# Wider weight units in a second mixer, and its last retention beside the output projection

## The chip, the cores and the metric

The kernel runs on one core of a Trainium2 chip. The metric is the device time of one execution in microseconds (us), as the median of several runs. One further execution is recorded by the hardware profiler; its trace gives the start and the length of every instruction on every engine: TensorE (PE, with its weight loads as PEld), VectorE (DVE), ScalarE (ACT), GpSimd (POOL), and SyncE (SP), which issues most of the transfers.

## What is computed

Two transformer blocks, one after the other, on 512 tokens of 1024 channels, in float32. The first block has a feed-forward, a mixer that ends in a product with `w_o`, and a second feed-forward. The second block has a mixer of latent attention and retention, and a layer of retrieved experts (`peer`). The change lies in the mixer of the second block; of the first block it touches the product with `w_o` alone.

```python
def hybrid_mixer(...):
    ...
    z = jax.nn.sigmoid(g_a) * (o_a @ w_up_a) + jax.nn.sigmoid(g_b) * (o_b @ w_up_b)
    return z @ w_o

def second_block(...):
    h = rms_norm_2(x, g_norm1[l]) * (1.0 + sc1) + sh1
    proj = h @ w_in[l]        # q_lat 256, kv_lat 128, k_rope 32, rq, rk, rv, rg 512 each
    y_mla = mla_group(q_lat, kv_lat, k_rope, ...)
    y_ret = retention_group(rq, rk, rv, rg, positions, g_ret_norm[l])
    mixed = jnp.concatenate([y_mla, y_ret], axis=-1) @ w_out[l]
    x = x + gt1 * mixed
    h2 = rms_norm_2(x, g_norm2[l]) * (1.0 + sc2) + sh2
    x = x + gt2 * peer(h2, ...)

def retention_group(q, k, v, gate, ...):     # 8 heads of 64, 4 chunks of 128 tokens
    ...
    scores = jnp.einsum('bnihd,bnjhd->bnhij', qc, kc) * dmask
    y_inner = jnp.einsum('bnhij,bnjhd->bnihd', scores, vc)
    ...                                      # states: prev of chunk n from chunks 0..n-1
    y_cross = jnp.einsum('bnihk,bnhkv,hi->bnihv', qc, prev, xi)
    y = (y_inner + y_cross)                  # then normalised per head, times silu(gate)
```

## The kernel before

**Products.** A float32 operand is held as a pair of rounded parts, high and low, and `mm3` (L124) makes a product of two such pairs with three matmuls (L126, L127, L128). Weights arrive by a transfer on SP's queue (`raw`, L109, two buffers) and are made into pairs by `split` (L116): ACT writes the high part (L120), DVE the low part (L121). Three pairs of 1024 columns are held at a time. Activations are turned by TensorE (`transposed`, L403, transposes in L414) and then made into pairs by `to_pair` (L130).

**Token tiles and banks.** The 512 tokens are four tiles of 128. PSUM has eight banks of 512 columns. They are dealt into rings: in the second mixer `ps` has four banks, `sc` two and `po` two (`self.banks(ps=4, sc=2, po=2)`). A tile of a ring is free again when its last reader is done.

**Dense units.** `nform` (L552) computes a unit: the token tile's transposed rows stand still, up to 256 weight columns stream past them, 8 steps over the 1024 channels, for the four token tiles in their four `ps` banks; then `then(t, p)` takes a bank's result away. `late` are two callbacks of the boundary before it, with which the last two token tiles are normalised and turned while the first products run.

**The second mixer** (`mixer2`, L1044). `mla` (L1077) computes the latents in two units (k latent with the rotated key part, 160 columns in a unit padded to 256; then the query latent, 256), norms and turns them, forms keys, values and queries, and does the causal attention (`heads_attend`, L925). Between its steps stand three units of the retention (`more`): values and gates of the heads' first half, values of the second half. The rest is the retention, done by halves of four heads. `ret_part` (L1136) is one unit of 256 columns (part 0 queries, 1 keys, 2 values, 3 gates); queries and keys are rotated (`rope`, L575), turned and put away. `ret_mix` does one half: the states of three chunks (L1188 to L1197), then for each chunk of 128 tokens the scores (L1207, masked in L1210), the output from the states (L1219, 64 rows of operand) and from the scores (L1220, 128 rows), alternating by head, squares (L1224), and the scaled output (L1232). `merge` (L635) runs the first half's `ret_mix` between the units of the second half (`ret_project`). The second half's `ret_mix` has beside it only the turning of the attention's output. After it all of PSUM is dealt into one ring, the retention's output is turned, and `project` does the output projection.

**Projection** (`project`, L1015). Eight half-units (512 channels by 256 columns). The first two are multiplied for all token tiles at once; the other six are kept as pairs, and `boundary` (L435) then finishes one token tile after the other: its products, the residual (L1633), the norm, and its transposes for the next layer. The first mixer's `w_o` goes through the same function. Its input `z` is made in eight rows, which come in the order 4, 5, 0, 6, 1, 7, 2, 3 (`combine1`, L965).

**Order.** What runs on one engine runs in an order that is fixed when the program is built: a scheduler takes the instruction that is ready first by its own estimate, and among those the one that stands first in the program.

## Time and profile before

| what | value |
|---|---|
| time, median of 3 runs | 2857.19 us (2850.86 to 2858.55) |
| profiled execution, its own time | 2857.06 us |
| its span in the trace | 2855.3 us |
| mean granted TensorE clock over the span | 0.987 of full speed |
| PE, PEld busy | 2786.9 us (98%), 2394.8 us (84%) |
| DVE busy | 2063.3 us (72%) |
| ACT busy | 1159.0 us (41%) |
| POOL busy | 368.6 us (13%) |

An engine's busy time is the sum of its instructions' times, and a share is of the span. The second mixer with its projection lies from about 1302 to 1598 us of the span. The granted clock is told as a share of the full 2.4 GHz: 1.00 is 2.4 GHz, 0.50 is 1.2 GHz, and a mean between them says that a stretch had both. A matmul's recorded time is that from its start to its end in the pipeline; what it costs in a run is the distance from its start to the start of the next.

### The profile page before, as it was taken

To read this page: it belongs to the slowest core of one execution; us is meant where nothing else is said; L and a number is where in the kernel's file an instruction comes from. 1 tells how busy PE (TensorE), PEld (TensorE's weight loads), DVE (VectorE), ACT (ScalarE), POOL (GpSimd) and SP (SyncE) were. 2 spreads that over 40 slices of the span, in tenths; PEclk is the share of its full clock that TensorE was granted. 3 is DMA by queue.
4 is the path that set the end of the run, shared out by engine and by line. 5 is a ranking of instruction groups with operands and counts; after the bars stand their busy time and mean duration, and the time that the engine had idled before them with its cause. 6 is when DMAs were issued, how large, how long until landed. Compare 5 with 4: busy or idle time off the path is not lost. (4 is left out here: it accounts for less than half of the span.)

```text
span 2855.3 us, 40921 instructions
## 1 busy us (share of the span) xinstructions
PE 2786.9 (98%) x15565; PEld 2394.8 (84%) x15565; DVE 2063.3 (72%) x4448; ACT 1159.0 (41%) x1930; POOL 368.6 (13%) x367
## 2 busy tenths in 40 slices
PE   8999999999999999999999999999999999999998
PEld 6877778869788877888898888999988888899996
DVE  6895257785656787226664789999967778887887
ACT  4343144333534444225522433655633333333333
POOL 0000000000000000001001002111121115443441
PEclk9999999999999999999997999999999999999999
DMA  6663221212033554321121226888899999888894
GB/s 274 224 232 140 94 84 60 93 60 89 16 139 139 188 225 178 110 103 42 67 79 47 103 90 216 310 281 309 322 333 338 327 313 362 314 311 319 295 334 189
DMA packets 152533, 553.08 MB, mean 194 GB/s; under 512 B 12368, under 2 KB 61840, under 8 KB 112400
## 3 DMA queue, kind: packets, MB, share of 16 engines
q1 hardware_dynamic: 111040, 404.25, 38.8%
q0 software_dynamic: 38848, 140.56, 13.8%
q10 hardware_dynamic: 2448, 5.65, 0.5%
q8 instruction: 122, 2.00, 0.3%
q14 instruction: 75, 0.61, 0.1%
HBM read 505.95 MB, written 44.47 MB: 193 GB/s over the span
## 5 line engine op out<-in xcount | busy, mean ns | idle before, releaser
L120 ACT ACTIVATE whi<-raw 128x1024 fp32r<-128x1024 f32 (+2 forms) x491 | 510.3, 1040 | 806.5 <-PE ps L127 377.3
L121 DVE TENSOR_TENSOR wlo<-raw,whi 128x1024 fp32r<-128x1024 f32 (+2 forms) x491 | 588.7, 1199 | 294.2 <-ACT whi L120 289.4
L126 PE MATMUL ps<-h_hi,whi 128*128 128x384 f32 (+2 forms) x1904 | 691.5, 364 | 4.6 <-ACT ga L1443 3.3
L127 PE MATMUL ps<-h_lo,whi 128*128 128x384 f32 (+2 forms) x1904 | 684.4, 360 | 0.9 <-DVE h_lo L132 0.9
L128 PE MATMUL ps<-h_hi,wlo 128*128 128x384 f32 (+2 forms) x1904 | 683.1, 359 | 1.6 <-DVE wlo L121 1.6
L126 PEld LDWEIGHTS ps<-h_hi,whi 128*128 128x128 f32 x1904 | 359.4, 189 | 37.7 <-ACT ga L1443 4.2
L128 PEld LDWEIGHTS ps<-h_hi,wlo 128*128 128x128 f32 x1904 | 359.1, 189 | 33.7 <-DVE wlo L121 2.4
L127 PEld LDWEIGHTS ps<-h_lo,whi 128*128 128x128 f32 x1904 | 359.7, 189 | 31.5 <-DVE h_lo L132 1.3
L126 PE MATMUL acc<-whi,wh 128*128 128x512 f32 x768 | 303.9, 396 | 1.6 <-ACT wh L131 1.6
L128 PE MATMUL acc<-whi,wl 128*128 128x512 f32 x768 | 303.9, 396 | 0.3 <-DVE wl L132 0.3
L127 PE MATMUL acc<-wlo,wh 128*128 128x512 f32 x768 | 303.7, 396 | 0.0
L1458 POOL DMA_INDIRECT erow<-in_eu,ids x128 | 142.8, 1116 | 649.3 <-DVE junk L1462 478.1
L131 ACT ACTIVATE wh<-wv 128x384 fp32r<-128x384 f32 x128 | 67.1, 524 | 339.4 <-issue 174.2
L1458 POOL DMA_INDIRECT erow<-in_ev,ids x128 | 166.7, 1302 | 222.7 <-DVE eacc L1470 197.0
L126 PE MATMUL ps<-whi,h_hi 128*128 128x256 f32 (+1 forms) x608 | 187.3, 309 | 0.0
L127 PE MATMUL ps<-wlo,h_hi 128*128 128x256 f32 (+1 forms) x608 | 185.3, 305 | 0.0
L128 PE MATMUL ps<-whi,h_lo 128*128 128x256 f32 (+1 forms) x608 | 185.2, 305 | 0.0
L128 PEld LDWEIGHTS acc<-whi,wl 128*128 128x128 f32 x768 | 144.5, 188 | 36.0 <-DVE wl L132 0.8
L126 PEld LDWEIGHTS acc<-whi,wh 128*128 128x128 f32 x768 | 144.3, 188 | 35.1 <-ACT wh L131 1.9
L127 PEld LDWEIGHTS acc<-wlo,wh 128*128 128x128 f32 x768 | 144.4, 188 | 32.9
L1470 DVE SCALAR_TENSOR_TENSOR eacc<-erow,wgt,eacc 128x1024 f32<-128x1024 f32 x127 | 162.7, 1281 | 4.0 <-DMA erow<-in_ev,ids 2.3
L285 DVE SCALAR_TENSOR_TENSOR rows<-mraw,sil,rows 128x256 f32<-128x256 f32 x336 | 160.3, 481 | 6.6
(457 smaller groups left out, 4602.9 us busy)
## 6 DMA issues: line engine op xcount, KB each, us to landing
raw<-in_euT SPq DMA_DIRECT2D x64, 1024.0 KB
raw<-in_evp SPq DMA_DIRECT2D x64, 1024.0 KB
raw<-in_gu SPq DMA_DIRECT2D x44, 1024.0 KB
mraw<-in_wmod SPq DMA_DIRECT2D x24, 1024.0 KB
mraw<-in_wada SPq DMA_DIRECT2D x24, 1024.0 KB
dg<-gb SPq DMA_DIRECT2D x24, 1024.0 KB
gt<-dg SPq DMA_DIRECT2D x16, 1536.0 KB
raw<-in_dn SPq DMA_DIRECT2D x22, 1024.0 KB
```

The source lines that it names most:

```text
L120: self.nc.scalar.activation(hi, r, AF.Copy)
L121: self.last_low = self.nc.vector.tensor_tensor(lo, r, hi.bitcast(F32), op=OP.subtract)
L126: mm(out, l[0], r[0], start=start, stop=False)
L127: mm(out, l[0], r[1], start=False, stop=False)
L128: self.last_mm = mm(out, l[1], r[0], start=False, stop=stop)
L131: self.nc.scalar.activation(hi, v, AF.Copy)
L285: nc.vector.scalar_tensor_tensor(rows, rv[:, k, :], c, rows, op0=OP.mult, op1=OP.add)
L1458: nc.gpsimd.indirect_dma_start(out=row, out_offset=None, in_=src, in_offset=bass.IndirectOffsetOnAxis(ap=ids[:, m:m + 1], axis=0))
L1470: nc.vector.scalar_tensor_tensor(eacc, row, wg[:, m:m + 1], eacc, op0=OP.mult, op1=OP.add)
```

## The change

Weights of the second mixer come in units of 416 or 512 columns, each as two halves of 512 channels (`half_units`).

- The two latent units become one of 416 columns (`latents`). The split of its last part goes into the space that later holds the values (`room`), and `cq2` and `oa2` share a space.
- The eight retention units of 256 columns become four of 512: values with gates (`ret_values`), queries with keys (`ret_queries`). Both halves' values and gates now stand inside `mla`. The rotation runs over eight heads at a time.
- `ret_mix` is split into `scores` and `outputs`. The scores of chunk n+1 come before the outputs of chunk n. An output chunk's products are grouped: scores' product of the first pair of heads, states' product of the first pair, states' product of the second pair, scores' product of the second pair. The bank rings are `sc` and `po` throughout. The states come after the first scores.
- The first half's `ret_mix` goes between the parts of the second half's query and key unit. The second half's goes beside the first quarter of the output projection (`project_start`: 512 channels of the attention by 512 columns, in eight parts of six matmuls); the retention's output is turned in the `po` banks as it comes.
- Both projections (`wo` and `wo2`) use half-units of 512 columns. In the second one `rest` turns the last token tile after the second quarter's products of the first two tiles have been put down; PSUM isn't dealt out anew.

The diff, cut to its core; most lines that go out are left out of it, since the functions before are printed above.

```diff
-            p = self.ps(tag)
+            p = self.ps(tag if isinstance(tag, str) else tag[k // 4])
...
+    def nform(self, *args, **kw):
+        for _ in self.nform_steps(*args, **kw):
+            pass
+    def nform_steps(self, units, x, width, then, kd=KD, late=None, room=None):
+        kr = kd // len(units)
+        kh = min(kr, 1024 // width)
         out = [self.ps() for _ in range(NT)]
         ws = []
+        for i, ap in enumerate(units):
+            r = self.raw(ap)
+            for k0 in range(i * kr, (i + 1) * kr, kh):
+                o = (k0 - i * kr) * width
+                end = k0 + kh == kd
+                hl = self.split(r[:, o:o + kh * width], [z[:, :kh * width] for z in room] if room and end else None)
+                ws += [(k0 + j, [z[:, j * width:(j + 1) * width] for z in hl]) for j in range(kh)]
+                if late and not end:
+                    continue
+                for t in range(NT):
+                    ts = slice(t * P, (t + 1) * P)
+                    if late and t < 2:
+                        late[t]()
+                    for k, w in ws:
+                        self.mm3(out[t][:, :width], (x[0][:, k, ts], x[1][:, k, ts]), w, k == 0, k == kd - 1)
+                    yield
+                ws = []
...
+    def project_start(self, ap, z, y):
+        r = self.raw(ap[0])
+        for i in range(2):
+            w = self.split(r[:, i * 1024:(i + 1) * 1024])
+            for t in range(NT):
+                self.project_part(z, y[t], t, 0, i, w)
+                yield
+    def project_part(self, z, o, t, u, i, w):
+        ts = slice(t * P, (t + 1) * P)
+        for j in range(2):
+            k = u // 2 * 4 + 2 * i + j
+            cs = slice(j * 512, (j + 1) * 512)
+            self.mm3(o, (z[0][:, k, ts], z[1][:, k, ts]), (w[0][:, cs], w[1][:, cs]), k == 0, k == KD - 1)
+    def project(self, ap, z, pool, join, scale, bias, y, rest=None, tags=("ps",) * NT):
         ws, room = [], []
+        for n, names in ((2, ("ath", "atl")), (1, ("bth", "btl"))):
+            q = [pool.tile([P, n, 1024], F32R, name=x, tag=x) for x in names]
+            room += [[v[:, j, :] for v in q] for j in range(n)]
+        for u in (1, 2, 3):
+            r = self.raw(ap[u])
+            for i in range(2):
+                ws.append((u, i, self.split(r[:, i * 1024:(i + 1) * 1024], room.pop(0) if len(ws) > 2 else None)))
+            if u == 1 and rest:
+                for t in range(2):
+                    for q in ws:
+                        self.project_part(z, y[t][1], t, *q)
+                rest()
+        def product(t):
+            for u, i, w in ws:
+                if not (rest and t < 2 and u == 1):
+                    self.project_part(z, y[t][u % 2], t, u, i, w)
+        return self.boundary(lambda t: join(t, y[t]), scale, bias, product, tags)
...
         oy = res.tile([P, NT, 512], F32, name="oy2")
+        x0, x1 = ({n: res.tile([P, NT, 256], F32, name=n + j) for n in "vg"} for j in "01")
+        more = [lambda: self.ret_values(0, x0, h), lambda: self.ret_values(1, x1, h)]
         with ExitStack() as s1:
+            oa = self.mla(self.pool(s1, "mla", reuse_waits="tile"), s1, res, h, late, more)
         with ExitStack() as s1:
             pool = self.pool(s1, "ret", reuse_waits="tile")
             self.ret_consts(pool)
             t1 = self.ret_tiles(pool, x1)
             with ExitStack() as s2:
                 t0 = self.ret_tiles(self.pool(s2, "ret0", reuse_waits="tile"), x0)
+                for _ in self.ret_queries(0, t0, h):
+                    pass
                 self.acol(4, 13, "g_norm2_2")
...
+                mix = self.ret_mix(0, t0, oy)
+                for n, _ in enumerate(self.ret_queries(1, t1, h)):
+                    if n % 2:
+                        next(mix, None)
+                for _ in mix:
+                    pass
             pool = self.pool(st, "turned2", side="right", reuse_waits="tile")
             mT = [pool.tile([P, KD, S], F32R, name=n) for n in ("mTh", "mTl")]
+            def turn(t):
+                self.transposed(oy[:, t, :], 4, t, *mT, self.col("g_ret_norm_2"), None, 4, tag="po")
+            for t in range(NT):
+                self.transposed(oa[:, t, :], 4, t, *mT, tag="sc")
+            y = [[self.ps()] for _ in range(NT)]
+            start = self.project_start(a["wo2"], mT, [z[0] for z in y])
+            for n, _ in enumerate(self.ret_mix(1, t1, oy)):
+                if n in (4, 6, 7):
+                    turn(n // 2 - 2 if n < 7 else 2)
+                next(start, None)
+            for _ in start:
+                pass
+        for t in range(2):
+            y[t].append(self.ps("sc"))
+        def rest():
+            turn(NT - 1)
+            for t in (2, 3):
+                y[t].append(self.ps("po"))
+        return mT, grow, y, rest, self.pool(st, "last2", reuse_waits="tile")
...
-        vv = pool.tile([P, NT, 512], F32, name="vv2")
         with ExitStack() as s2:
             prep = self.pool(s2, "prep2", reuse_waits="tile")
             pa = prep.tile([P, NT, 416], F32, name="pa2")
+            cq = res.tile([P, 4, S], F32R, name="cq2", tag="oa2")
+            cq = [cq[:, :2], cq[:, 2:]]
             ck = [prep.tile([P, 1, S], F32R, name=n) for n in ("ckh2", "ckl2")]
-            self.latents(a["wi2"][0], 160, h, pa, 0, late)
+            room = pool.tile([P, 2, 1024], F32R, name="room2", tag="vv2")
+            self.latents([a["wi2"][j] for j in range(2)], 416, h, pa, 0, late, [room[:, j, :] for j in range(2)])
+            vv = pool.tile([P, NT, 512], F32, name="vv2", tag="vv2")
             self.banks(ps=4, sc=2, po=2)
             for t in range(NT):
                 c = pa[:, t, 0:128]
                 self.normed(c, 128)
                 self.transposed(c, 1, t, ck[0], ck[1], self.col("g_kv_norm_2"), tag="sc")
-            self.latents(a["wi2"][1], 256, h, pa, 160)
-            more[0]()
-            w = self.split(self.raw(a["wl5"]))
             for t in range(NT):
                 c = pa[:, t, 160:416]
                 self.normed(c, 256)
                 self.transposed(c, 2, t, cq[0], cq[1], self.col("g_q_norm_2"), tag="sc")
+            more[0]()
+            w = self.split(self.raw(a["wl5"]))
             self.k_nope([w], 1, ck, kT)
             for t in range(NT):
                 ts = slice(t * P, (t + 1) * P)
...
+            self.q_rope(a["wl4"], 2, cq, qT, None, 4)
             more[1]()
-            self.q_rope(a["wl4"], 2, cq, qT, None, 4)
-            more[2]()
             self.q_nope(a["wl3"], 2, cq, qT)
...
+    def ret_units(self, hh, n):
+        return [self.a["wr2"][(2 * hh + n) * 2 + j] for j in range(2)]
+    def ret_values(self, hh, x, h):
+        nc = self.nc
+        def then(t, p):
+            pv = p[:, :256].rearrange("p (h e) -> p h e", e=64)
...
+            nc.scalar.activation(x["g"][:, t, :], p[:, 256:], AF.Silu)
+        self.nform(self.ret_units(hh, 1), h, 512, then)
+    def ret_queries(self, hh, x, h):
+        nc = self.nc
+        zeta = self.rc["zeta"]
+        xi = self.rc["xi"].rearrange("p (g i) -> p g i", g=4)[:, 2 * hh:2 * hh + 2]
+        def then(t, p):
             ts = slice(t * P, (t + 1) * P)
+            qr = self.misc.tile([P, 8, 64], F32, name="rr", tag="v")
+            self.rope(p.rearrange("p (h e) -> p h e", e=64), qr, 32, 4 + t, 8)
+            nc.vector.tensor_tensor(x["kz"][:, t, :].rearrange("p (h e) -> p h e", e=64), qr[:, 4:],
+                                    zeta[:, 4 * hh:4 * hh + 4, None].to_broadcast([P, 4, 64]), op=OP.mult)
             pp = self.ps("sc")
+            for g in range(4):
                 nc.tensor.transpose(pp[:, g * P:(g + 1) * P],
                                     qr[:, 2 * g:2 * g + 2, :].rearrange("p a b -> p (a b)"), self.idf)
+            pv = pp.rearrange("p (n g e) -> p n g e", g=2, e=P)
+            nc.scalar.activation(x["qT"][:, :, ts], pv[:, 0], AF.Copy)
+            nc.scalar.activation(x["kT"][:, :, ts], pv[:, 1], AF.Copy)
+            nc.vector.tensor_tensor(x["qx"][:, :, ts], pv[:, 0], xi, op=OP.mult)
+        yield from self.nform_steps(self.ret_units(hh, 0), h, 512, then)
+    def ret_mix(self, hh, x, oy):
         nc = self.nc
         st = x["st"]
         dm = self.rc["dmask"].rearrange("p (g s i) -> p s g i", g=4, s=2)[:, :, 2 * hh:2 * hh + 2]
         dec = self.rc["dec"][:, 2 * hh:2 * hh + 2]
+        half = [slice(64 * s, 64 * s + 64) for s in range(2)]
+        ats = {}
+        def scores(n):
             ts = slice(n * P, (n + 1) * P)
+            ats[n] = self.misc.tile([P, 4, P], F32, name="rat", tag="sg")
+            pst = [self.ps("sc"), self.ps("sc")]
             for g in range(2):
                 for s in range(2):
+                    nc.tensor.matmul(pst[s][:, g * P:(g + 1) * P], x["kT"][half[s], g, ts], x["qT"][half[s], g, ts],
                                      start=True, stop=True)
             for s in range(2):
+                nc.vector.tensor_tensor(ats[n][:, 2 * s:2 * s + 2, :],
+                                        pst[s][:, :256].rearrange("p (g i) -> p g i", g=2), dm[:, s], op=OP.mult)
+        def outputs(n):
+            ts = slice(n * P, (n + 1) * P)
+            at = ats.pop(n)
+            py = [self.ps("po"), self.ps("po")]
+            o = [[py[s][:, g * 64:(g + 1) * 64] for s in range(2)] for g in range(2)]
+            def inner(g, start):
+                for s in range(2):
                     hd = 2 * g + s
+                    nc.tensor.matmul(o[g][s], at[:, 2 * s + g, :], x["v"][:, n, hd * 64:(hd + 1) * 64],
+                                     start=start, stop=not n or not start)
+            def cross(g, start):
+                for s in range(2) if n else ():
+                    nc.tensor.matmul(o[g][s], x["qx"][half[s], g, ts], st[half[s], n - 1, g, :],
+                                     start=start, stop=not start)
+            inner(0, True)
+            cross(0, False)
+            cross(1, True)
+            inner(1, not n)
...
+        scores(0)
+        for n in range(3):
+            p = self.ps("po")
+            for g in range(2):
+                gs = slice(g * P, (g + 1) * P)
+                nc.tensor.matmul(p[:, gs], x["kz"][:, n, gs], x["v"][:, n, gs], start=True, stop=True)
...
+        yield
+        for n in range(NT):
+            if n + 1 < NT:
+                scores(n + 1)
+                yield
+            outputs(n)
...
-            h = self.project(a["wo"], z, pool, pn(1), 2, 6)
+            y = [[self.ps(), self.ps()] for _ in range(NT)]
+            for _ in self.project_start(a["wo"], z, [q[0] for q in y]):
+                pass
+            h = self.project(a["wo"], z, pool, pn(1), 2, 6, y)
...
-            mT, grow, pool = self.mixer2(h[0], st, h[1])
-            h = self.project(a["wo2"], mT, pool, lambda t, y: self.residual(t, y, grow), 4, 12)
+            mT, grow, y, rest, pool = self.mixer2(h[0], st, h[1])
+            h = self.project(a["wo2"], mT, pool, lambda t, y: self.residual(t, y, grow), 4, 12, y, rest,
+                             [("ps", "sc" if t < 2 else "po") for t in range(NT)])
...
+    def half_units(w, n):
+        return np.concatenate([cols_units(w[q * 512:(q + 1) * 512], n) for q in range(2)])
...
-    a["wo"] = cols_units(f["w_o"][0], 256)
+    a["wo"] = half_units(f["w_o"][0], 512)
-    a["wi2"] = cols_units(w2, 256)
+    a["wi2"] = half_units(np.concatenate([w2[:, 256:416], w2[:, :256]], 1), 416)
+    r2 = w2[:, 416:].reshape(D, 2, 2, 2, 256).transpose(0, 3, 1, 2, 4).reshape(D, 4, 512)
+    a["wr2"] = np.concatenate([half_units(r2[:, n], 512) for n in range(4)])
-    a["wo2"] = cols_units(f["w_out_2"][0], 256)
+    a["wo2"] = half_units(f["w_out_2"][0], 512)
```

## Rows read from the trace of the kernel before

**Rows 1.** page, section 1: busy us, share of span, instructions

```profile
PE 2786.9 (98%) x15565; PEld 2394.8 (84%) x15565; DVE 2063.3 (72%) x4448; ACT 1159.0 (41%) x1930; POOL 368.6 (13%) x367
```

**Rows 2.** stretches: from:to, us, busy (instructions) by engine, granted clock, DMA share, GB/s

```profile
1301.70:1322.30 20.60, 15.67 (x114) 15.47 (x113) 12.99 (x41) 11.19 (x29) 3.49 (x8) 0.83 0.14 52
1473.40:1550.90 77.50, 72.42 (x442) 64.25 (x441) 42.40 (x136) 19.04 (x40) 10.17 (x16) 0.78 0.09 32
1550.90:1597.90 47.00, 47.00 (x402) 47.00 (x401) 28.13 (x49) 19.46 (x31) 1.65 (x3) 1.00 0.27 101
```

**Rows 3.** PE's waits, 1300 to 1600: us in total, times, longest

```profile
PE ps L414 <- DVE oy L1232: 3.1, 1, 3.1
```

**Rows 4.** PE by time, latents (start, us, instruction): twelve starts apart

```profile
1328.11 0.28 PE L127 MATMUL ps<-wlo,h_hi 128*128 128x256 f32 x1
...
1329.55 0.28 PE L127 MATMUL ps<-wlo,h_hi 128*128 128x256 f32 x1
```

**Rows 5.** PE by time, second feed-forward's down projection: eight starts apart

```profile
1299.62 0.39 PE L126 MATMUL ps<-fhi,lhi 128*128 128x512 f32 x1
...
1301.44 0.39 PE L128 MATMUL ps<-fhi,llo 128*128 128x512 f32 x1
```

**Rows 6.** PE by time, last token tile's transposes at the latents, wait

```profile
1310.50 1.97 PE L414 MATMUL ps<-idf,xs 128*128 128x128 f32 x8 [4.93 <-ACT xs L448]
```

**Rows 7.** PE by time, first output projection: a wait; two starts 36 apart

```profile
875.62 0.38 PE L126 MATMUL ps<-whi,zh 128*128 128x256 f32 x1 [1.02 <-ACT zh L131]
...
880.22 0.28 PE L126 MATMUL ps<-whi,zh 128*128 128x256 f32 x1
...
884.46 0.28 PE L126 MATMUL ps<-whi,zh 128*128 128x256 f32 x1
```

**Rows 8.** PE by time, retention: merged lines (xcount) with the next start

```profile
1473.39 0.60 PE L1163 MATMUL sc<-idf,rr 128*128 128x128 f32 x4
1473.83 1.06 PE L1188 MATMUL po<-v,rkz 128*128 128x128 f32 x8
...
1481.60 0.56 PE L1220 MATMUL po<-v,rat 128*128 128x64 f32 x4
1481.97 0.36 PE L127 MATMUL ps<-wlo,h_hi 128*128 128x256 f32 x1
...
1505.10 0.69 PE L1219 MATMUL po<-rst,rqx 64*128 64x64 f32 x2
1505.71 0.69 PE L1220 MATMUL po<-v,rat 128*128 128x64 f32 x2
...
1516.99 0.71 PE L1207 MATMUL sc<-rqT,rkT 64*128 64x128 f32 x8
1517.54 0.34 PE L1219 MATMUL po<-rst,rqx 64*128 64x64 f32 x4
1517.71 0.44 PE L1207 MATMUL ps<-rqT,rkT 64*128 64x128 f32 x2
1518.21 0.43 PE L1220 MATMUL po<-v,rat 128*128 128x64 f32 x2
1518.58 0.43 PE L1219 MATMUL po<-rst,rqx 64*128 64x64 f32 x2
```

**Rows 9.** busy time of 5 us slices of the retention

```profile
1500.00:1505.00 5.00, 5.00 (x22) 4.34 (x21) 2.03 (x7) 0.28 (x1) 1.28 (x2) 0.50 0.02 3
1530.00:1535.00 5.00, 5.00 (x23) 4.24 (x23) 2.21 (x7) 0.56 (x2) 1.05 (x3) 0.54 0.00 0
```

**Rows 10.** ACT, DVE by time; DVE groups: count, busy us, mean ns

```profile
1544.63 0.28 ACT L1224 ACTIVATE ysq<-ps 128x128 f32<-128x128 f32 x1 [1.38 <-PE ps L1220]
1546.83 0.86 DVE L1232 SCALAR_TENSOR_TENSOR oy<-ps,rstd,rg 128x64 f32<-128x64 f32 x4 [1.47 <-POOL rstd L148]
...
L121 DVE TENSOR_TENSOR wlo<-raw,whi 128x1024 fp32r<-128x1024 f32 x5 | 6.1, 1220 | 0.0
L1159 DVE TENSOR_TENSOR rkz<-rr,zeta 128x256 f32<-128x256 f32 x8 | 3.4, 423 | 0.2
```

154 lines of the change are left out of this document (25 added, 129 removed).

## The prediction, made before the changed kernel had run

> **What bounds the kernel now.** I read the busy time of each engine first, then a table of stretches around the second mixer, then who TensorE (PE) waited for there, then PE's instructions in order of time, for the distance from one start to the next. PE is busy for 98% of the span [rows 1], so time goes where PE's own instructions go, or where its clock falls. The table cuts the stretch that is changed into four parts [rows 2]: the end of the feed-forward boundary with the first latent unit (20.6 us), the attention part with the second latent unit and three retention units (to 1473.4, not among the rows), the retention (77.5 us), the output projection (47.0 us). The reader is to see the third row: 72.4 us busy, but the mean granted clock is 0.78, DVE is busy for only 42.4 us, and DMA hardly at all. PE is the limit there too, with poor work: small matmuls, partly at 1.2 GHz instead of 2.4. The waits it has, the longest 3.1 us [rows 3], come to 77.5 - 72.4 = 5.1 us. After this mixer the kernel is a chain of PE work whose gathers and loads are issued by its progress; I see no transfer with a date of its own, so I let what is saved here reach the end in full.
>
> **Paces of the wide matmuls.** A start with 256 columns comes every 1.44/12 = 0.120 us [rows 4], one with 512 every 1.82/8 = 0.2275 us [rows 5]. The distance is not proportional: two narrow ones take 0.240, so joining them gives back 0.0125 us. Between the two a straight line gives 0.187 us for 416 columns (estimate). In the first mixer's output projection the narrow ones come every 4.24/36 = 0.1178 us [rows 7], so less is gained there.
>
> **Latent units (160 of 256 columns, then 256; now 416).** Before, 192 matmuls of 256 columns: 23.0 us. After, 96 x 0.187 = 18.0. On the path it is more: 24 of them for the first token tile lie ahead of the wait for the last token tile's normalised rows [rows 6], which ends when ACT and DVE are done, so they are filler there; behind it 168 x 0.120 = 20.2 become 72 x 0.187 = 13.5, -6.7 us. Four splits of 832 columns stand ahead of that chain where two of 1024 stood; one of them lies in the chain of ACT and DVE and costs between 0 and 1.0 us (1.2 us for 1024 columns [rows 10], scaled); I take 0.6. Sum -6.1. The clock after the wait is a further open point: the stretch has 0.83 [rows 2], so 0.17 x 20.6 = 3.5 us at most are lost to it. A wait shorter by 1.6 us might keep it; I count nothing, and 2.4 us in the low end. The second latent unit hid the chain of the key-value norm; now the value unit does, 21.8 us of independent matmuls, and the instructions on PE are ordered by readiness, so that costs nothing. If the value unit's splits came late (their buffers come free within the last token tile, 4.5 us, against 2.3 for a split on both engines), it would be some 2 us.
>
> **Retention units (eight of 256 become four of 512).** Each pair goes from 192 x 0.120 = 23.0 to 96 x 0.2275 = 21.8: -1.2 each, -4.8 us. The second half's gates move from the retention into the attention stretch, which changes no sum. The rotation now runs over eight heads in one instruction; DVE has half as many, of about 0.42 us [rows 10] instead of two of 0.28, and gains some. But it holds a bank of the four until its four reads are done, and then() of four token tiles takes about 10 us against 8.2 until the next unit wants the last bank: a wait of about 1.5 us, counted below.
>
> **Output projections (256 to 512 columns).** The first: 384 x 0.1178 = 45.2 becomes 192 x 0.2275 = 43.7, -1.5. Its first products needed rows 0 to 3 of z at once and waited 1.02 us for the last [rows 7]; now 24 matmuls (5.5 us) need rows 0 and 1 alone, and rows 2 and 3, the last to be made, have arrived by then: -1.0 (0 if the order is otherwise). The second by the same paces -0.7 to -1.5; I take -1.0.
>
> **Retention.** Of the 77.5 us, 288 matmuls of 0.120 are 34.6; 42.9 are scores, states, outputs, transposes and waits. Prices at full clock: 8 score instructions 0.55, 4 full-row output instructions 0.37, 4 half-row ones behind half-row ones 0.17 [rows 8]. When half-row and full-row pairs alternate, a pair takes 0.37 [rows 8], twice the price of a pair in a run: a change between the two costs about 0.2. Before, an output chunk with a state has eight such pairs, 2.9 us; grouped it is 0.37 + (0.2 + 0.34) + 0.37 = 1.28. One half of the heads is then 3 x 1.28 + 0.74 + 4 x 0.55 + 12 state instructions at 0.11, taken from the transposes of the same width [rows 8], = 8.1 us, both 16.2; 48 transposes at 0.11 5.3; entering and leaving the 16 steps between dense products 16 x 0.2 = 3.2: 24.7 us at full clock, against 42.9, -18.2.
>
> Full clock is the condition. It is 1.2 GHz from 1500 on and again from soon after 1530 [rows 9], each time after PE had run the scores and outputs without dense products between; a pair then takes 0.61 [rows 8]. After the change every step of the last half has 6 products of 512 columns (1.37 us) beside it, eight of them, and 24 more ahead of the last turn. I expect 2.4 GHz to hold.
>
> What is given back: DVE. Its work in this stage (42.4 us, plus about 5 for splits that now fall in it) meets a PE that needs 21.8 + 24.7 + 10.9 + 5.5 = 62.9 us, and the later part, from the end of the last query unit on, is nearly even: some 45 us on DVE against 48 on PE. Also the outputs, the turns and the states share two banks, so a chunk can start only when the last one's rows are turned. From square to the end of the scaled output takes 1546.83 + 0.86 - 1544.63 = 3.1 us [rows 10], with outputs, transposes and the four scalings some 6. Queued behind a wait of PE for such a bank are the dense products, in the order fixed when the program was built. The trace shows no such wait, so it is bounded: 2 us (the one bank wait above) to 16 (4 us in each of four chunks); I take 6, nearest to the 5.1 that PE waited in this stage before. Retention: -18.2 + 6 = -12.2. The wait of 3.1 us for the last turned rows [rows 3] goes, since 5.5 us of attention products lie over it.
>
> **Sum.** -6.1 - 4.8 - 1.5 - 1.0 - 1.0 - 12.2 = -26.6 us, against the profiled execution's 2857.06 us (span 2855.3; the median of three is 2857.19, so no correction): 2830 us.
>
> **Rivals.** (1) The clock falls in the last retention all the same, because the dense steps are run early, while DVE still rotates, and the small work stands bare at its end. For: PE's order follows readiness, and the steps are ready early. Price: some 10 us of small work at 0.61 for 0.37, +5, and the wait for the last rows back, +3: 2838 us. (2) Wide products gain less than the rows say.
>
> In the rows a 256 takes 0.120 us and a 512 0.2275 [rows 4, 5]. The Trainium skill ("TensorE: Matmul & The Clock Gate", Back-to-back issue gap) gives the gap of a lone stream as N/2.4 + 2.5 ns, by which joining two 256s saves 2.5 ns and not 12.5, and the 768 joined pairs give an estimated 1.9 us in place of the 7.3 above. The trace does not agree with it.
>
> If joining saved nothing but the padding, latents would give -5, the units and projections -1.0 (the wait) and retention -12.2: 2839 us. The shorter distance of narrow matmuls in the first projection [rows 7] speaks for it. (3) More: the clock holds after the first wait and waits in the retention are 2 us: 2824. (4) Slower: the two shared banks. If every chunk of both halves waits out its chain of some 6 us, because the fillers were placed elsewhere, that is 8 x 4 = 32 us instead of 6, and with such gaps the clock is at 1.2 GHz for the dense steps too, 16.4 us of products that then take 29: -26.6 + 26 + 13 = +12, 2869. It turns into a loss where the waits pass some 25 us. Against it: DVE is idle for almost half of the stage [rows 2], and all of PE's waits there are 5.1 us. (5) In between, with 12 to 20 us more in waits: 2842 to 2850.
>
> **How the numbers follow.** Forecast 0.57, rival 1 0.16, rival 2 0.05, rival 3 0.06, rival 5 0.10, rival 4 0.06. A measurement of this kernel tells some 0.3% (8.6 us) from no change. Faster takes the forecast and rivals 1 to 3 (all at least 18 us below) and a little of rival 5's 2842 to 2850: 0.86; same most of the rest of it: 0.09; slower 0.05. The range: the low end takes the best bounds (-8.5, -4.8, -1.5, -1.0, -1.5, -16.2: 2824) less the 4 us by which executions lie from their median, 2819; the high end takes rivals 1 and 2 and half of 5: 2847.
>
> **What would show it.** In the profile after: starts of 512 columns every 0.2275 us in the retention units and about 0.187 for 416; the row of the retention stage with a clock near 1.00; output instructions in runs of four; no wait of the transposes for the scaled outputs; the start of the attention products between them. Wrong would be: a clock of 0.5 for over 5 us in that stage (rival 1), PE waits for DVE or for the output banks of over 10 us in sum (rivals 4 and 5), or an unchanged time per column in the wide units (rival 2).

## The result, and the profile after

The changed kernel takes 2831.6 us (median of 4 runs, 2829.14 to 2834.26) where the kernel before took 2857.57 beside it: a ratio of 0.9912, 95% interval 0.9901 to 0.9924, 26.0 us less. The prediction was 2830, 2819 to 2847. In a later set on another occasion the same kernel gave 0.9900 (0.9885 to 0.9915). The profiled executions differ by 2855.3 - 2829.2 = 26.1 us, so the traces can be laid side by side.

The page of after, section 1 (busy us, share of the span, instructions), which answers to [rows 1]:

```profile
PE 2760.7 (98%) x14699; PEld 2334.1 (83%) x14701; DVE 2058.3 (73%) x4398; ACT 1154.3 (41%) x1927; POOL 368.3 (13%) x367
```

PE is as full as before and has 26.2 us less to do; the others have hardly changed. Now the stretches of the second mixer in after, against [rows 2] (from:to, us, busy and instructions of PE, PEld, DVE, ACT, POOL, granted clock, DMA share, GB/s): the boundary with the latents; the rest of the attention's dense work with both value units; the two query units with most of the first half's retention; its end with the rotations; the second half's retention beside the projection; the rest of the projection. The attention itself, between the second and the third, is left out here and follows further down.

```profile
1298.76:1320.75 21.99, 20.52 (x113) 19.52 (x112) 15.22 (x42) 13.90 (x31) 3.48 (x8) 1.00 0.22 85
1320.75:1386.98 66.23, 62.66 (x290) 49.29 (x289) 45.61 (x111) 27.00 (x54) 4.76 (x10) 1.00 0.27 92
1435.86:1493.20 57.34, 57.31 (x307) 46.47 (x306) 31.53 (x80) 12.31 (x26) 7.17 (x12) 1.00 0.27 95
1493.20:1511.20 18.00, 11.14 (x62) 9.44 (x63) 14.34 (x46) 5.89 (x14) 1.37 (x2) 0.72 0.00 1
1511.20:1541.10 29.90, 28.88 (x169) 22.50 (x167) 18.30 (x45) 8.76 (x16) 6.05 (x8) 1.00 0.17 64
1541.10:1571.25 30.15, 30.15 (x143) 24.75 (x143) 21.36 (x42) 14.71 (x26) 1.64 (x3) 1.00 0.26 100
```

Two rows stand out. The fifth is what was hoped for: half the retention beside dense products, PE busy for 28.9 of 29.9 us, clock 1.00. The fourth is a hole: PE busy for 11.1 of 18 us, a mean clock of 0.72, and DVE, at 14.3 of 18, the busier one. PE's waits from 1436 to 1545 name what it waited for there (us in total, times, longest):

```profile
PE sc L1216 <- DVE rr L598: 4.3, 2, 2.6
PE po L1287 <- DVE oy L1278: 2.2, 1, 2.2
PE po L414 <- DVE oy L1278: 1.0, 2, 0.7
PE po L1255 <- DVE oy L1278: 0.4, 1, 0.4
```

L1216 are the transposes of the rotated queries and keys, L598 the last step of the rotation: the largest wait is for the rotation of the second query unit, not for the banks. The others, 3.6 us together, are for banks of the ring `po`.

To see which part of the change brought what, each stage is taken from a mark on PE to the next, in both traces. The mark at either end of the second mixer is the turning of the third token tile's normalised rows (L414, `xs`): 1301.67 to 1597.96 before, 1298.76 to 1571.25 after, 296.3 and 272.5 us. The first output projection runs from its first product to the same turning behind it; before, then after:

```profile
871.01 0.28 PE L126 MATMUL ps<-whi,zh 128*128 128x256 f32 x1
...
920.48 1.03 PE L414 MATMUL ps<-idf,xs 128*128 128x128 f32 x8
```

```profile
870.77 0.39 PE L126 MATMUL ps<-whi,zh 128*128 128x512 f32 x1
...
916.93 1.03 PE L414 MATMUL ps<-idf,xs 128*128 128x128 f32 x8
```

| stage | before | after | difference | predicted |
|---|---|---|---|---|
| first output projection | 49.5 | 46.2 | -3.3 | -2.5 |
| boundary, latents, dense work up to the attention's first scores | 86.3 | 88.2 | +1.9; a unit of 11.5 us moved here, so -9.6 | -8.5 |
| from there to the third turning behind the projection | 210.0 | 184.3 | -25.7; without that unit -14.2 | -15.6 |
| all else | | | +1.0 | 0 |
| sum | | | -26.1 | -26.6 |

The unit of 11.5 us is the second half's gates, 96 matmuls at 0.120 [rows 4]. The last line of differences, +0.6 between the two mixers, +0.6 behind the second, -0.2 ahead of the first, is in code that wasn't changed. It isn't explained. Inside the second mixer the scores' new order (a chunk ahead of the outputs) has no run of its own below; it is part of the -25.7.

### The profile page after: what moved, and what is told of

The parts are those of the page before. It is cut to its first block, busy times and chain, and to the rows that moved or that the text cites. A ratio compares the mean times of both kernels' runs of the same rounds, so it can differ in the third digit from the quotient of the medians.

```text
span 2829.2 us, 39121 instructions
## 1 busy us (share of the span) xinstructions
PE 2760.7 (98%) x14699; PEld 2334.1 (83%) x14701; DVE 2058.3 (73%) x4398; ACT 1154.3 (41%) x1927; POOL 368.3 (13%) x367
## 5 line engine op out<-in xcount | busy, mean ns | idle before, releaser
L120 ACT ACTIVATE whi<-raw 128x1024 fp32r<-128x1024 f32 (+3 forms) x490 | 508.8, 1039 | 797.6 <-PE ps L127 386.3
L121 DVE TENSOR_TENSOR wlo<-raw,whi 128x1024 fp32r<-128x1024 f32 (+3 forms) x490 | 586.6, 1198 | 292.4 <-ACT whi L120 290.0
L126 PE MATMUL ps<-h_hi,whi 128*128 128x384 f32 (+2 forms) x1904 | 691.5, 364 | 4.0 <-ACT ga L1511 2.4
L126 PEld LDWEIGHTS ps<-h_hi,whi 128*128 128x128 f32 x1904 | 359.5, 189 | 37.2 <-ACT ga L1511 3.3
L126 PE MATMUL acc<-whi,wh 128*128 128x512 f32 x768 | 303.7, 396 | 1.9 <-ACT wh L131 1.9
L131 ACT ACTIVATE wh<-wv 128x384 fp32r<-128x384 f32 x128 | 67.1, 524 | 340.4 <-issue 171.8
L126 PEld LDWEIGHTS acc<-whi,wh 128*128 128x128 f32 x768 | 144.3, 188 | 35.3 <-ACT wh L131 2.2
L132 DVE TENSOR_TENSOR wl<-wv,wh 128x384 fp32r<-128x384 f32 x128 | 71.2, 556 | 123.3 <-ACT wh L131 123.3
L1530 DVE SCALAR_TENSOR_TENSOR junk<-erow,xr 128x1024 bf16<-128x1024 f32 x128 | 155.1, 1217 | 6.3 <-DMA erow<-in_eu,ids 6.1
L126 PE MATMUL ps<-whi,h_hi 128*128 128x384 f32 (+3 forms) x440 | 153.3, 349 | 0.6 <-DVE rt L596 0.6
```

Of the source, the lines that this page charges most:

```text
L120: self.nc.scalar.activation(hi, r, AF.Copy)
L121: self.last_low = self.nc.vector.tensor_tensor(lo, r, hi.bitcast(F32), op=OP.subtract)
L126: mm(out, l[0], r[0], start=start, stop=False)
L131: self.nc.scalar.activation(hi, v, AF.Copy)
L132: self.last_pair = self.nc.vector.tensor_tensor(lo, v, hi.bitcast(F32), op=OP.subtract)
L1530: nc.vector.scalar_tensor_tensor(junk, row, 1.0, xr, op0=OP.mult, op1=OP.mult, accum_out=act[:, m:m + 1])
```

## The experiments

All but one are the changed kernel with one thing undone or added; `grouped` is the kernel before with one thing added. The ratio is to the kernel before in the same set; the length is that of the second mixer between the two marks in its own trace, which tells a few us apart where medians hardly do.

| run | median us | ratio (95%) | second mixer, us |
|---|---|---|---|
| before | 2857.57 | | 296.3 |
| after, and again | 2831.6, 2829.92 | 0.9912 (0.9901 to 0.9924), 0.9900 (0.9885 to 0.9915) | 272.5, 272.9 |
| serial | 2849.59 | 0.9972 (0.9961 to 0.9983) | 292.6 |
| grouped | 2854.42 | 0.9989 (0.9977 to 1.0) | 294.9 |
| alternate | 2839.08 | 0.9934 (0.9920 to 0.9947) | 280.6 |
| halves | 2837.88 | 0.9933 (0.9920 to 0.9946) | 277.9 |
| latents | 2840.03 | 0.9933 (0.9920 to 0.9947) | 281.7 |
| tail | 2831.42 | 0.9907 (0.9894 to 0.9920) | 273.8 |
| fill | 2827.11 | 0.9889 (0.9874 to 0.9904) | 269.9 |
| fill0 | 2819.6 | 0.9871 (0.9847 to 0.9895) | 265.1 |
| batch | 2830.7 | 0.9903 (0.9880 to 0.9927) | 273.2 |
| fill0b | 2822.24 | 0.9882 (0.9855 to 0.9909) | 265.8 |

The changed kernel beside three of them, `after_again`:

> The changed kernel itself, beside the others of this set on one chip. 2830 to 2833 us; the same hole between 1495 and 1510 us.

It repeats the first result, hole and all: 272.9 us, 7.9 us of waits from the attention's end to the end of the projection, as in the first trace. Its 2829.92 us lie just under the range expected.

### The cover: serial

```diff
-            for n, _ in enumerate(self.ret_mix(1, t1, oy)):
-                if n in (4, 6, 7):
-                    turn(n // 2 - 2 if n < 7 else 2)
-                next(start, None)
+            for t, _ in enumerate(self.ret_mix(1, t1, oy)):
+                if t < NT:
+                    self.transposed(oa[:, t, :], 4, t, *mT, tag="sc")
+        self.banks(ps=8)
+        for t in range(NT):
+            self.transposed(oy[:, t, :], 4, t, *mT, self.col("g_ret_norm_2"), None, 4)
```

> The changed kernel, but its last retention has only the turning of the attention's output beside it; the retention's output is then turned and the whole projection follows, as in the kernel before. Theory (the clock holds because dense products stand between the small ones): PE's small work of the last half, 12.7 us at full clock in the changed kernel, falls to 1.2 GHz and takes some 8 us more, and the waits come back, 5 us instead of 1.0: +12 us over the changed kernel, some 2844 us, with a granted clock near 0.5 for over 10 us ahead of the projection. Rival (the products would have filled PE just as well afterwards, only the wait for the last rows returns): +3 us, 2835 us, with the clock near 1.00.

292.6 us in the second mixer, +20.1 against after; the ratio says 17 to 21 us. The edit takes the cover away and also brings back the new dealing of PSUM's banks before the projection. Its stretches (columns as above):

```profile
1500.00:1510.00 10.00, 4.30 (x20) 3.32 (x20) 7.94 (x26) 1.32 (x4) 0.51 (x1) 0.69 0.01 2
1510.00:1530.00 20.00, 20.00 (x75) 16.58 (x74) 10.88 (x28) 3.50 (x8) 2.54 (x4) 0.50 0.00 0
1530.00:1550.00 20.00, 14.75 (x58) 12.60 (x58) 9.07 (x28) 3.71 (x8) 2.53 (x4) 0.55 0.02 7
```

From 1510 to 1530 PE is never idle and still at 1.2 GHz: 75 instructions where a like stretch of after has over a hundred. The theory holds and its price was too low: waits 12.1 us in place of 7.9, and the distances of the small matmuls (scores, outputs, states, transposes) 51.3 us in sum in place of 33.4. Products that run beside the retention and products that run after it are not the same time, because the small work alone doesn't keep 2.4 GHz: here the clock was down from 1503.7 to 1548.1.

### The order of the products: alternate and grouped

`alternate` puts the old order into the changed kernel:

```diff
-            inner(0, True)
-            cross(0, False)
-            cross(1, True)
-            inner(1, not n)
+            for s in range(2):
+                for g in range(2):
+                    hd = 2 * g + s
+                    if n:
+                        nc.tensor.matmul(o[g][s], x["qx"][half[s], g, ts], st[half[s], n - 1, g, :], start=True, stop=False)
+                    nc.tensor.matmul(o[g][s], at[:, 2 * s + g, :], x["v"][:, n, hd * 64:(hd + 1) * 64],
+                                     start=not n, stop=True)
```

> The changed kernel, but the half-row and the full-row products of each output chunk alternate by head again, as before. Theory (a change between half-row and full-row products costs PE about 0.2 us): by the prediction's prices +1.6 us in each of six chunks, +9.7 us; by the changed kernel's own trace, where a grouped chunk costs 1.85 us and not 1.28, +1.1 each, +6.7 us: 2838 us, all of it in the distances of these products and none in waits. Rival (the price of an alternating pair in the kernel before was the fallen clock, not the change between them): under +2 us, 2833 us.

One chunk in after, by time on PE (start, us, instruction), with the start of what follows it, 1490.22 - 1488.68 = 1.54 us:

```profile
1488.68 0.56 PE L1255 MATMUL po<-v,rat 128*128 128x64 f32 x4
1489.16 0.66 PE L1260 MATMUL po<-rst,rqx 64*128 64x64 f32 x8
1489.76 0.66 PE L1255 MATMUL po<-v,rat 128*128 128x64 f32 x4
1490.22 0.48 PE L126 MATMUL ps<-whi,h_hi 128*128 128x512 f32 x1
```

and the same chunk in `alternate`, eight pairs in 2.79 us, 0.36 each but for the last, as the alternating pairs of [rows 8]:

```profile
1489.42 0.43 PE L1268 MATMUL po<-rst,rqx 64*128 64x64 f32 x2
1489.78 0.43 PE L1269 MATMUL po<-v,rat 128*128 128x64 f32 x2
...
1491.96 0.43 PE L1269 MATMUL po<-v,rat 128*128 128x64 f32 x2
1492.21 0.48 PE L126 MATMUL ps<-whi,h_hi 128*128 128x512 f32 x1
...
1493.13 0.63 PE L126 MATMUL ps<-whi,h_hi 128*128 128x512 f32 x1
1493.56 0.63 PE L127 MATMUL ps<-wlo,h_hi 128*128 128x512 f32 x1
```

Both chunks stand between dense products. The difference is 1.25 us for seven changes between the kinds inside the chunk where the grouped one has two, about 0.25 us a change. That the price is the change between the two kinds is shown here at full clock. Over all six chunks it is less than six times 1.25: in the last two, dense products stand between the two halves of a chunk, and a half takes 1.09 us in after,

```profile
1526.31 0.33 PE L1255 MATMUL po<-v,rat 128*128 128x64 f32 x2
...
1527.40 0.48 PE L126 MATMUL ps<-whi,mTh 128*128 128x512 f32 x1
```

and 1.33 in `alternate`:

```profile
1532.49 0.43 PE L1268 MATMUL po<-rst,rqx 64*128 64x64 f32 x2
...
1533.82 0.48 PE L126 MATMUL ps<-whi,mTh 128*128 128x512 f32 x1
```

Summed from PE's distances, the output products take 5.8 us more (18.4 for 12.6). The second mixer is 8.1 us longer: dense products 2.8 more, the other small ones 1.8 more, waits 2.3 less. So the theory's +6.7 is near, but not all of the 8.1 is in these products. The Trainium skill ("TensorEngine Tiling (Array Packing)", Key Properties) says that changing the tiling mode drains the engine, without a figure; the trace agrees in that a change costs time, about 0.25 us, and no run shows whether it is a drain. The last two lines of that chunk's view show something more: after 2.8 us of alternating, the dense products themselves ran at 1.2 GHz for 3.4 us (0.43 us from start to start), with no wait before them.

`grouped` does that part alone, in the kernel before:

```diff
-            for s in range(2):
-                rows = slice(64 * s, 64 * s + 64)
-                for g in range(2):
+            for g, kind in ((0, 0), (0, 1), (1, 1), (1, 0)):
+                for s in range(2):
```

> The kernel before with the grouped order of the output products alone. Theory (the change between half-row and full-row products costs by itself, at either clock): six chunks, 1.1 us each at full clock as the changed kernel's trace has it, more at half clock, less what waits come instead: -6 us against the kernel before, 2850 us, between -10 and -3. Rival (the grouping pays only where dense products hold the clock): -2 to 0 us, 2855 us.

Here the rival is nearer: -1.4 us by the trace, -3 by the ratio, its interval from -6.6 to 0. The clock in three stretches:

```profile
1494.00:1509.00 15.00, 15.00 (x74) 14.05 (x74) 4.44 (x13) 4.01 (x8) 2.55 (x4) 0.54 0.03 4
1514.00:1523.00 9.00, 8.82 (x46) 7.70 (x45) 5.04 (x17) 1.75 (x5) 1.27 (x2) 0.62 0.00 0
1529.00:1547.00 18.00, 13.47 (x63) 12.35 (x64) 8.85 (x31) 3.50 (x8) 3.77 (x6) 0.53 0.00 0
```

The clock was at 0.50 for 37.5 us (1494.9 to 1508.5, 1515.3 to 1522.2, 1529.0 to 1546.1), where the kernel before had 34.1 (1499.7 to 1513.4 and 1530.4 to 1550.9; [rows 9] are a slice of each). The output products did get cheaper, 20.4 us for 23.3, but the waits took back 1.1 and the states 1.0. The products came closer together and the clock was down for longer; that the one follows from the other is not shown. So `alternate` and `serial` don't add up: 8 us for the order and 20 for the cover share the same clock, and the order alone is worth 1 to 3.

### The widths: halves and latents

`halves` issues each product of 512 columns as two of 256:

```diff
+    def mm3h(self, out, l, r, start, stop):
+        ...
+        for c in cs:
+            if not start:
+                mm(out[:, c], l[0], r[0][:, c], start=False, stop=False)
+            mm(out[:, c], l[0], r[1][:, c], start=False, stop=False)
+            self.last_mm = mm(out[:, c], l[1], r[0][:, c], start=False, stop=stop and c is cs[1])
```

> The changed kernel, but the products of 512 columns in the retention's units and in both projections are issued as two of 256 (the first of each bank stays whole); everything else stays. The latents' 416 columns stay too. Theory (a 256 costs 0.120 us and a 512 costs 0.2275): 768 joined pairs come apart, +4.8 for the units, +1.5 and +0.7 for the projections, some +7 us, 2838.5 us. Rival (joining gives back only the fixed gap of a stream, 2.5 ns in each pair by the page of the Trainium skill that the prediction names): +1.9 us, 2833.5 us.

By the traces +1.4 us in the first projection (870.45 to 918.02, 47.6 for 46.2), +2.2 up to the attention, +2.9 from there to the end of the second projection: 6.5 us; by the ratios 6 to 9. In the second of these parts the clock was at 0.50 for 3.4 us (1325.3 to 1328.7), which it wasn't in after; that is worth up to 1.7 us, half of its length, and PE waited 0.9 us less there. So the widths come to some 5 to 6 us. That is nearer to the theory's +7 than to the rival's +1.9. The rule of the Trainium skill that the prediction weighed would make it an estimated 1.9 us ("TensorE: Matmul & The Clock Gate", Back-to-back issue gap); the trace doesn't agree.

`latents` has the two units of 256 back:

```diff
-            self.latents([a["wi2"][j] for j in range(2)], 416, h, pa, 0, late, [room[:, j, :] for j in range(2)])
+            self.latents([a["wi2"][0]], 160, h, pa, 0, late)
...
+            self.latents([a["wi2"][1]], 256, h, pa, 160)
```

> The changed kernel with the latents as two units of 256 columns (160 of them used in the first) as before, all else as changed. By the prediction's term +6.1 us; by the two traces +7.2 (10.1 us more in the stage of the boundary and the latents, 3.0 us less in waits of the key-value norm behind it): 2838 to 2839 us, the wait of 4.9 us for the last token tile's rows and a mean clock of 0.83 back. Rival (only the 96 columns of padding count, the wait was filled by chance): +5 us or less, with a wait under 2 us and the clock at 1.00.

+9.2 us in the second mixer. The wait for the last token tile's rows, first in `latents`, then in after, with the products that follow in after; twelve starts of 416 columns take 1309.46 - 1307.20 = 2.26 us, 0.188 each:

```profile
1308.91 1.97 PE L414 MATMUL ps<-idf,xs 128*128 128x128 f32 x8 [4.93 <-ACT xs L448]
```

```profile
1306.08 1.09 PE L414 MATMUL ps<-idf,xs 128*128 128x128 f32 x8 [0.53 <-ACT xs L448]
...
1307.20 0.35 PE L127 MATMUL ps<-wlo,h_hi 128*128 128x416 f32 x1
...
1309.46 0.35 PE L127 MATMUL ps<-wlo,h_hi 128*128 128x416 f32 x1
```

The eight transposes take 1.97 us at half clock in the one and 1.09 in the other. All of the products of a token tile, 24 x 0.188 = 4.5 us, now lie over the wait, where 24 narrow ones took 2.9; the chain of ACT and DVE is 1.5 us shorter as well, 0.9 of it because ACT scales the last rows (L448) ahead of the third tile's pairs (L131) and no longer behind them; and the clock no longer falls.

### The hole: tail, fill, fill0

Three runs separate the late rotations from the missing cover. `tail` does the last two parts of a query unit together, tile by tile, with the rotation at once:

```diff
+                if (late or tail and i == len(units) - 1) and not end:
                     continue
...
+                    if tail and end:
+                        then(t, out[t][:, :width])
```

> The changed kernel, but the last two parts of each query unit are done together, token tile by token tile, and a tile's rotation follows at once, so that the four rotations start some 3 us apart instead of all after the last part. Theory (the hole of the changed kernel between 1495 and 1510 us, 6.5 us of PE waits for the rotation and 10 us at half clock, comes because all four rotations become ready within the last part): -5 us against the changed kernel, 2826.5 us, between -9 and 0, and no stretch at a clock of 0.5 there. Rival (VectorE's work in this stretch is the limit, whatever its order): within 1.5 us of the changed kernel.

`fill0` leaves the rotations late and brings dense products: the attention's half of the projection's input has a space of its own, is turned before the second query unit, and the projection's first quarter begins beside the end of the first half's retention.

```diff
             t1 = self.ret_tiles(pool, x1)
+            pool = self.pool(st, "turned2", side="right", reuse_waits="tile")
+            mT = [pool.tile([P, 4, S], F32R, name=n) for n in ("mTh", "mTl")]
...
+                for t in range(NT):
+                    self.transposed(oa[:, t, :], 4, t, *mT, tag="sc")
                 mix = self.ret_mix(0, t0, oy)
...
-                for _ in mix:
-                    pass
+                y = [[self.ps()] for _ in range(NT)]
+                start = self.project_start(a["wo2"], mT, [z[0] for z in y])
+                for _ in mix:
+                    next(start, None)
```

> The changed kernel with only the second half of the run called fill: the attention's half of the projection's input in a space of its own, turned before the second query unit, and the projection's first quarter started beside the end of the first half's retention; the rotations come as late as in the changed kernel. With the runs tail (early rotations alone) and fill (both) this separates the two causes of the hole. Theory (the missing cover is the larger cause, and the small work stays spread over all sixteen steps of the query unit): no stretch at 0.5 over 3 us after 1490 us, waits of 3 to 5 us, -5 us against the changed kernel, 2825 us. Rival (the projection's products need the banks that the late rotations hold, so they start no earlier and the hole stays): within 1.5 us of the changed kernel, 2829 to 2832 us.

`fill` is both:

> The changed kernel with the last parts of the query units done tile by tile as in the run before, and besides with the attention's half of the projection's input in a space of its own, so that it is turned before the second query unit and the eight parts of the projection's first quarter start beside the end of the first half's retention. Theory (the hole has two causes, late rotations and no dense products to stand over them; the run with early rotations alone lost its shorter waits again to 13 us at half clock): waits of 2 to 4 us in place of 7.9 and no stretch at 0.5 between 1490 and 1515 us, -8 us against the changed kernel, 2823 us, between -11 and -4. Rival (the last chunks, whose cover is moved forward, now stand bare at the end and lose as much): within 2 us of the changed kernel, with the half clock moved to 1520 us or later.

| | rotations late | rotations early |
|---|---|---|
| no cover | after: waits 7.9 us, second mixer 272.5 | tail: waits 5.0, 273.8 |
| cover | fill0: waits 1.8, 265.1 | fill: waits 3.1, 269.9 |

The waits are those of PE from the attention's end to the mark behind the projection. One stretch of each, `tail`, `fill`, `fill0`:

```profile
1496.50:1510.00 13.50, 12.29 (x45) 9.98 (x46) 6.94 (x19) 3.01 (x7) 2.64 (x4) 0.50 0.13 54
```

```profile
1510.50:1516.50 6.00, 6.00 (x20) 4.62 (x21) 3.18 (x12) 0.00 (x0) 1.26 (x2) 0.50 0.00 0
```

```profile
1490.00:1520.00 30.00, 28.39 (x169) 22.04 (x168) 22.25 (x70) 6.31 (x16) 5.27 (x8) 1.00 0.13 46
```

Early rotations without cover shorten the waits by 2.9 us and give them back: the second query unit has twelve steps instead of sixteen to spread the first half's work over, the small work that stood behind the rotations comes sooner, nothing dense is left beside it, and PE is at half clock for 13.5 us. The theory for `tail` falls; the rival's result is right, though not by its reason, since DVE is now idle for half of that stretch. With cover alone the products stand over the rotations, the waits fall to 1.8 us, and the clock is 1.00 throughout: -7.4 us in the second mixer, more than the -5 expected. The products do need banks that the rotations hold, but the first is free at 1494.4 and that is early enough. With both, the twelve steps remain; scores and outputs bunch at 1506 to 1510 and the clock falls behind them for 6.8 us, though a like bunch in `fill0` kept 1.00. The cause of the hole is settled as far as these runs go: with the rotations as late as before, cover alone takes it away. Early rotations with the work still spread over sixteen steps weren't tried. `fill0` is faster than either kernel: 0.9871 of before.

### The waits behind the latents: batch, fill0b

Behind the latents after has new waits. From 1320 to 1340:

```profile
PE sc L414 <- DVE v L427: 2.1, 3, 1.3
PE sc L414 <- DVE pa L164: 0.7, 1, 0.7
```

`batch` norms and turns the latents for all four token tiles at once:

```diff
-                self.normed(c, 128)
-                self.transposed(c, 1, t, ck[0], ck[1], self.col("g_kv_norm_2"), tag="sc")
...
+                r = self.rstd(ms, 4)
+                c = pa[:, :, at:at + n * P]
+                nc.vector.tensor_tensor(c, c, r[:, :, None].to_broadcast([P, NT, n * P]), op=OP.mult)
+                for k in range(n):
+                    p = self.ps("sc")
+                    for t in range(NT):
+                        nc.tensor.transpose(p[:, t * P:(t + 1) * P], pa[:, t, at + k * P:at + (k + 1) * P], self.idf)
```

> The changed kernel with the norms of the latents made for all four token tiles at once (one reciprocal root, one product, one bank of transposes for each 128 latent columns) in place of tile by tile. Theory (the 3 us of new waits behind the latents come from twelve transposes that stand in PE's order among the value unit's products and wait one by one for VectorE, which has the unit's splits ahead of them): the waits of transposes for the latents, 2.9 us in sum, fall under 1 us, -3 us, 2827 us. Rival (the last token tile's chain is as long as before, and PE waits for it once instead of four times): within 1 us.

The rival holds: one wait in place of several, of about the same length (2.7 us in after).

```profile
PE sc L1149 <- DVE pa L1145: 3.0, 1, 3.0
```

The last token tile's chain is what PE waits for, and the order fixed on PE puts its transposes ahead of products that were ready. How long the wait would be with the transposes later in that order wasn't tried. Behind the one wait the clock was at 0.50 for 3.4 us (1325.8 to 1329.2), which it wasn't in after, so what `batch` saves elsewhere can't be read from its time.

> The two edits of this set together. If both theories hold, the sum of the two differences, some -8 us against the changed kernel, 2822 us; if the late rotations keep the hole, -3 us, 2827 us.

265.8 us in the second mixer, as `fill0` alone (265.1): the batch adds nothing there either, and the 2822 us expected come from the cover alone.

## Why the prediction was right, and where it wasn't

**What bounds it.** PE's own distances and its clock, as the prediction had it: nothing saved in the mixers was lost further on. The first projection's 3.3 us and the second mixer's 23.8 reach the end but for the 1.0 that stays open.

**Wide products.** Units and projections were to give 4.8 + 1.5 + 0.7 to 1.0; `halves` gives 6.5, and some 5 to 6 without the fall of the clock in it. The straight line's 0.187 us for 416 columns was measured as 0.188. Rival 2 falls.

**First projection, the waits.** -1.0 was taken for the last row of `z`. Of the 3.3 us measured 1.4 are the width; the other 1.9 are that wait, a second one, which the prediction left out, and slow starts beside them. PE's waits of the kernel before from 862 to 928, both gone after:

```profile
PE ps L126 <- ACT zh L131: 1.0, 1, 1.0
PE ps L128 <- DVE zl L132: 0.6, 1, 0.6
```

**Latents.** The term was -6.1. The boundary's stage gained more: the wait fell from 4.93 to 0.53 us with another 0.9 at a split, where the prediction took it to be shorter by 1.6; and the clock held, which it named as open and left out, with 2.4 us in the low end (rival 3's first half). The other way went the chain of the key-value norm, which the value unit was to hide at no cost: three splits of that unit, 3.5 us on DVE, stood ahead of the last tile's copy and norm, and PE waited 2.7 us for it, 1.2 before. The prediction had named late splits at some 2 us and counted nothing. That is the step that failed: of a moved unit its splits count too, on the engine that the chain runs on. Together, 9.2 us by the run.

**Retention.** The net was right, -12.2 against -11.3 (25.7 - 11.5 - 2.9 of the widths), but two errors cancel in it. The prediction took 288 wide products for the stretch from 1473.4 to 1550.9. One of the three lines of `mm3` alone (L126), from the attention's end and then in that stretch of the kernel before (PE and PEld, then clock, DMA share and GB/s):

```profile
1435.30:1473.40 38.10, 27.39 (x96) 18.38 (x96) 1.00 0.31 106
1473.40:1550.90 77.50, 20.05 (x64) 13.77 (x65) 0.78 0.09 32
```

Three units, 288 products, had run ahead of it, and 192 are in it. So 77.5 - 192 x 0.120 = 54.5 us were small work, waits and lost clock, not 42.9. The sum for after was too low by as much, some 43 us for 24.7 + 6: outputs, scores and states 22.4 for 16.2, the 48 transposes 7.3 for 5.3, the waits 7.9 for 6, and what the dense products took beyond 0.2275 us each, some 5 for 3.2. Each side was some 12 us too low, so the difference came out; that is luck.

The parts of the net, summed from PE's distances between the attention's end and the projection's: scores -4.0 us, the two kinds of output products -10.7, states and transposes 0, waits +2.9. The price of the change between the kinds was right (2.79 us a chunk for the 2.9 assumed), the grouped chunk is a little dearer than assumed (1.54 for 1.28), and a part of it all was at half clock. The dense products gained another 1.0 us. The attention ahead, which wasn't changed, is 1.5 us longer; from its first scores to its last product, before and after:

```profile
1387.98:1436.63 48.65, 46.39 (x340) 37.76 (x339) 29.76 (x90) 27.97 (x83) 0.00 (x0) 1.00 0.07 23
1386.98:1437.13 50.15, 47.88 (x338) 39.08 (x337) 29.83 (x90) 28.10 (x83) 0.00 (x0) 0.97 0.07 23
```

It has the same wait of 2.3 us in both, and behind it the clock is at 0.50 for 3.4 us (1390.6 to 1394.0) in after alone. Every run with the changed kernel has this, `grouped` and the kernel before don't; why the same wait costs the clock in one and not in the other is open.

The condition, 2.4 GHz, held where the prediction argued for it, in the eight steps of the last half (clock 1.00 from 1511 to 1541). It fell where the prediction didn't look for it, at the end of the first half's retention, for 10.2 us; that is over the 5 us in this stage that the prediction itself named as a sign of being wrong. In all, the second mixer was at half clock for 41.0 us before, 13.7 after, 47.8 in `serial` and 3.4 in `fill0`. The 6 us given back were put on the two shared banks; these cost 3.6 us, and the rotation of the second query unit, which the prediction had only as 1.5 us of waiting for a bank, cost 4.3. So rival 1's mechanism (small work bare, the clock down) happened in another place and at a lower price than its 8 us, and rival 4's hardly: 3.6 us of bank waits against the 25 from which it would have lost. That the sum came within 2 us is in large part luck: beside the two errors of the retention, the stages missed by -0.8, -1.1, +1.4 and +1.0, which leaves 0.5, and inside the second one some -4 of the boundary stand against the 2.7 of new waits.

## What to carry to other kernels

A saving on small matmuls is worth its price list only while the clock is up: the same regrouping gave 8 us with dense products around it and 1 to 3 without. So ask of each stretch of small work which dense products can stand beside it, and give these a place in memory early enough; here 16 KB per partition for the turned half of an input, taken a stage sooner, were worth another 7 us. And where a unit is moved to hide a chain, look at what it puts on the engines of that chain.

## What the runs showed of the hardware

A busy PE isn't enough for 2.4 GHz. In `serial` it was busy without a gap from 1510 to 1530 and stayed at 0.50, after a fall at 1503.7 that came behind waits. In `alternate` the clock fell behind 2.8 us of alternating half-row and full-row products that had dense products on both sides and no wait; this happened behind the chunks at 1489.42 and 1523.92, and not behind the one at 1480.10. In `fill` it fell behind 4 us of scores and outputs, also without a wait. In these places of `alternate` and `fill` small matmuls stood in front, not idle time. How many are too many isn't settled: in `fill0` 6.6 us of small work with only four products of 512 columns in it (1503.95 to 1510.53) kept 1.00, where a like 6.4 us of `fill` with three (1503.88 to 1510.24) ended in the fall. With the dense products brought forward, as in `fill0`, the clock was at 1.00 from 1391.9 to the end of the second mixer. The Trainium skill ("TensorE: Matmul & The Clock Gate", HAM oscillation — how this bites in real kernels) ties such falls to stretches in which PE waits; the falls in `alternate` and `fill` had no wait in front, so it doesn't cover them. Nor does a wait settle it: in the attention one of 2.3 us was followed by a fall after the change and by none before it.
